# Hybrid Conformer and stick-breaking block: zero block kept in tiles, second convolution buffer, gate results on ScalarE's queue, last merged block by halves

## Chip, core and metric

The kernel runs on one core of a Trainium2 chip. The metric is the device time of one execution in microseconds (us), taken as the median of several runs. The kernel before takes 1413.03 us (three runs, 1412.89 to 1413.87).

Engines are named as in the profile: PE is TensorE (matmuls), PEld its weight loads, DVE is VectorE, ACT is ScalarE, POOL is GpSimd, SP is SyncE. Transfers are issued from the queues of SP and POOL in the kernel before, and all run on 16 DMA engines.

## What is computed

One layer of a decoder trunk on a sequence of 1024 tokens with 1024 channels, in float32. Each sub-layer is framed by RMSNorms and by a shift, scale and gate that come from a conditioning vector. The first sub-layer runs two mixers on the same input, merges them by gates, and projects:

```python
proj = h @ w_in
glu_in, qkv, gates = jnp.split(proj, [2 * CONV_WIDTH, 2 * CONV_WIDTH + 3 * ATT_WIDTH], axis=-1)
u_val, u_gate = jnp.split(glu_in, 2, axis=-1)
u = causal_depthwise_conv(u_val * jax.nn.sigmoid(u_gate), conv_w, conv_b)      # 31 taps
y_conv = jax.nn.silu(layernorm(u, conv_ln_g, conv_ln_b)) @ w_conv_out
o = stick_breaking_attention(q, k, v)                                          # 8 heads of 64
y_att = o @ w_att_out
g_conv, g_att = jnp.split(gates, 2, axis=-1)
merged = jax.nn.sigmoid(g_conv) * y_conv + jax.nn.sigmoid(g_att) * y_att
return merged @ w_o
```

Stick-breaking attention has a weight for each pair of a query t and an earlier key s (s < t, strictly): sigmoid of the score times the product of sigmoid(-score) over the keys between s and t. Weights of keys at or after the query are zero. The second sub-layer is a SwiGLU feed-forward block.

## The kernel before

All matmuls that need float32 accuracy are made of three: both operands are split into a high part in float32r and a low part (the rest), and high x high, high x low and low x high are summed in PSUM. A split is an ACT copy for the high part and a DVE subtraction for the low part. This pair of instructions stands behind nearly every operand.

The work runs in stages. The times are those of the profiled execution.

1. From 0 to about 75 us the input is normed and modulated, and the first projections are made as the operands arrive.
2. From about 75 to 430 us there is attention, with other projections as filler. Line 598 goes over four pairs of heads; each pair calls `glu` (line 417), `conv` for the group before (line 438) and `attend` (line 582), which runs `head` (line 514) twice and, between, `qk_pair` for the next pair. `head` has a higher priority, so the planner takes its instructions first and fills PE's time with the projections, the convolution and the plain gate (line 606).
3. Still inside the same scope come 14 early gate products. `early(i, q)` (line 615) computes for each of seven gate pairs two products that need only the modulated input, accumulated in one PSUM bank `k`; after the first (q = 0) and after the second (q = 1) an ACT instruction evicts the bank to a tile `ee` (tag `sg`, two buffers, line 623), and `store` (line 625) sends it to DRAM on POOL's queue. The second product of a pair adds to the bank, so it must follow the first eviction. The order is early(0, 0), early(1, 0), early(0, 1), early(2, 0) and so on.
4. From line 664 on, the rest of each gate pair is made in a form of Strassen's: sums of blocks of the modulated input, T1 to T4, are loaded again from DRAM (tiles `f`, `s`, `x`), combined on DVE (lines 674 to 677) and split (`make_t`, line 657). `other_five` (line 696) makes the five products of a pair from them. The convolution's LayerNorm (`ln_all`), its projection and the attention's projection follow.
5. At line 830 a loop over n = 0 to 7 merges the two mixers channel block by channel block. Each block has two halves of 512 tokens (c = 0, 1); for each half, DVE multiplies the projection by its gate and adds it to the convolution's part, tile `y`. After both halves the block of 1024 columns is split into `mhi` and `mlo` (line 842, `split_r`).
6. From line 954 the output projection `pwo` runs over these blocks for c = 0 first. From there on the FFN follows, up to the end at 1413 us; the change doesn't touch it.

**Order.** `TileContext(schedule_with_timeline_sim=True)` (line 1811) lets a planner set the order of the instructions on each engine: by priority, and by a modelled timeline of when operands and buffers are free. Two stretches of the code are pinned to the written order (`pin`, line 174: the start and the beginning of the FFN); the stages 2 to 5 are not. Each engine then runs its own list in order, so an instruction that waits holds all behind it on its engine. SP's and POOL's queues are such lists too.

**Diagonal blocks in `head`.** The 1024 x 1024 weights of a head are made by rows of queries: for each c (four per head) two query blocks of 128, ii = 0 and 1, over all keys up to them. For the product with the values the weights must be transposed, key by query, in steps of two key blocks (jp; jj = 0 and 1). Lines 559 to 576 do this for one step: four transposes of 128 x 128 on PE fill one PSUM bank `tr` of 512 columns, ACT evicts it to `ahi`, DVE writes the rest to `alo`, and four matmuls of 256 columns add to `av`. On the diagonal (jp = c), key block 1 lies after query block 0, so its weights are zero; the kernel transposes a tile of zeros there (line 564) to keep the layout:

```python
src = zeros if (jp == c and jj == 1 and ii == 0) else probs[ii][:, jo:jo + P]
```

There are 80 steps in all, 32 of them on the diagonal. `ahi` and `alo` have two buffers each.

**The convolution.** `glu(ct)` writes its product `u` to DRAM (`v_d`, line 436). `conv(ct)` (line 438) loads it back in another layout as `ph` (line 441), with four extra columns per group that POOL sets to zero (line 440), and runs 80 small matmuls `pcv` over it with five weight tiles `cvw` (tag `wraw`, three buffers). `ph` has one buffer, so the load for group ct waits until the products of group ct - 1 are through.

[...]

Of the kernel before, what the change touches and what calls it, by code (L numbers as in the profile page):

```python
# [69 lines left out]
def tile_block(ctx: ExitStack, tc: tile.TileContext, xT, vecs, ada1, ada2, win, wv, wcv, wat, wo, w1, w2, cvw, out):  # L70
# [29 lines left out]
    def store(dst, src):  # L100
        nc.gpsimd.dma_start(dst, src)
# [5 lines left out]
    make_identity(nc, ident)  # L107
    ones = small.tile([P, P], F32, name="ones")
    pool.memset(ones, 1.0)
    zeros = small.tile([P, P], F32, name="zeros")  # L110
    pool.memset(zeros, 0.0)
    eps = small.tile([P, 1], F32, name="eps")
    pool.memset(eps, EPS)

# [292 lines left out]
    with ExitStack() as sC:  # L407
        pc = mkpool(sC, "pc")
        with ExitStack() as sA:
# [4 lines left out]
            pool.memset(eye, 0.0)  # L414
            pool.tensor_copy(eye[:, CH - P:], ident)

            def glu(ct):
                u = pc.tile([P, T], F32, tag="u", name=f"u{ct}", bufs=1)
                u_mr = u.rearrange("p (r m) -> p m r", r=PH)
                sgs = list(sg0) if ct == 0 else []  # L420
                if ct:
                    w = load_w(win[4 + ct], f"wgg{ct}")
                    gb = banks2(f"pgg{ct}")
                    gemm(gb, w, h, range(KT))
                for c in range(NCH if ct else 0):
                    sg = sgp.tile([P, CH], F32, tag="sg", name=f"sg{ct}_{c}", bufs=2)
                    act.activation(sg, gb[c], AF.Sigmoid, bias=0.0, scale=1.0)
                    sgs.append(sg)
                w = load_w(win[ct], f"wgv{ct}")
                vb = banks2(f"pgv{ct}")  # L430
                gemm(vb, w, h, range(KT))
                for c in range(NCH):
                    ms = slice(c * (CH // PH), (c + 1) * (CH // PH))
                    vr, sr = (t.rearrange("p (m r) -> p m r", r=PH) for t in (vb[c], sgs[c]))
                    dve.tensor_tensor(u_mr[:, ms], vr, sr, op=ALU.mult)
                load(channels(v_d[ct]), u)

            def conv(ct):
                ph = pc.tile([P, NG, SH - 1 + TM], F32, tag="ph", name=f"ph{ct}", bufs=1)
                pool.memset(ph[:, :, 0:SH - 1], 0.0)  # L440
                load(ph[:, :, SH - 1:], v_d[ct].rearrange("g p m -> p g m"))
                wts = []
                for hf in range(2):
                    cv = bank(f"pcv{ct}_{hf}")
                    o = sgp.tile([P, NG // 2, TM], F32, tag="sg", name=f"co{ct}_{hf}", bufs=2)
                    for gi in range(NG // 2):
                        g = hf * (NG // 2) + gi
                        for d in range(SH):
                            n, at = divmod((g * SH + d) * P, T)
                            if n == len(wts):  # L450
                                wts.append(wp.tile([P, T], F32, tag="wraw", name=f"cvw{ct}_{n}"))
                                load(wts[n], cvw[ct, n])
                            pe.matmul(cv[:, gi * TM:(gi + 1) * TM], wts[n][:, at:at + P],  # L453
                                      ph[:, g, SH - 1 - d:SH - 1 - d + TM], start=(d == 0), stop=(d == SH - 1))
                    for gi in range(NG // 2):
                        b = C_CB + ct * NG + hf * (NG // 2) + gi
                        act.activation(o[:, gi], cv[:, gi * TM:(gi + 1) * TM], AF.Identity, bias=vec[:, b:b + 1],
                                       scale=1.0)
                    load(u_d[ct][hf * (NG // 2):(hf + 1) * (NG // 2)].rearrange("g p m -> p g m"), o)
# [54 lines left out]
            def head(p, hh, qst, kst, klo, vts, oT):  # L514
# [6 lines left out]
                for ci, c in enumerate(order):  # L521
# [5 lines left out]
                    for sc in range(nsc - 1, -1, -1):  # L527
                        probs = []
                        for i in (2 * c, 2 * c + 1):
                            W = P * (i + 1)  # L530
                            if i not in kaps:
                                kaps[i] = pa.tile([P, T], F32, tag="kap", name=f"ka{tag}_{i}", bufs=2)
                            kap = kaps[i]
                            s_lo, s_hi = sc * CH, min(W, (sc + 1) * CH)
                            w = s_hi - s_lo
                            beta = pa.tile([P, CH], F32, tag="beta", name=f"be{tag}_{i}_{sc}", bufs=4)
                            tcols = slice(i * P, (i + 1) * P)
                            z = psz.tile([P, CH], F32, tag="z", name=f"z{tag}_{i}_{sc}")
                            z_lo = s_lo if w >= 256 else max(0, s_hi - 256)
                            z_hi = max(s_hi, z_lo + 256)  # L540
                            zw, zo = z_hi - z_lo, s_lo - z_lo
                            diag = s_hi == W
                            pe.matmul(z[:, :zw], qst[:, tcols], kst[:, z_lo:z_hi], start=True, stop=False)
                            pe.matmul(z[:, :zw], qst[:, tcols], klo[:, z_lo:z_hi], start=False, stop=True)  # L544
                            act.activation(kap[:, s_lo:s_hi], z[:, zo:zo + w], AF.Sigmoid, bias=0.0, scale=-0.125)  # L545
                            m = w - 1 if diag else w
                            act.activation(beta[:, :m], z[:, zo:zo + m], AF.Sigmoid, bias=0.0, scale=0.125)  # L547
                            rev = kap[:, s_lo:s_hi][:, ::-1]
                            if diag:
                                pool.memset(beta[:, m:w], 0.0)  # L550
                                dve.tensor_tensor_scan(rev, rev, eye[:, CH - w:][:, ::-1], 0.0, op0=ALU.mult,  # L551
                                                       op1=ALU.add)
                            else:
                                dve.tensor_tensor_scan(rev, rev, rev, kap[:, s_hi:s_hi + 1], op0=ALU.mult,  # L554
                                                       op1=ALU.bypass)
                            dve.tensor_tensor(beta[:, :m], beta[:, :m], kap[:, s_lo + 1:s_lo + 1 + m], op=ALU.mult)  # L556
                            probs.append(beta)
                        for jp in range(min(c, 2 * sc + 1), 2 * sc - 1, -1):
                            tr = pst.tile([P, CH], F32, tag="tr", name=f"tr{tag}_{c}_{jp}")
                            for jj in range(2):  # L560
                                j = 2 * jp + jj
                                for ii in range(2):
                                    jo = (j - 4 * sc) * P
                                    src = zeros if (jp == c and jj == 1 and ii == 0) else probs[ii][:, jo:jo + P]
                                    o = jj * 256 + ii * P
                                    pe.transpose(tr[:, o:o + P], src, ident)  # L566
                            ahi = pa.tile([P, CH], F32R, tag="ahi", name=f"ahi{tag}_{c}_{jp}", bufs=2)
                            alo = pa.tile([P, CH], F32R, tag="alo", name=f"alo{tag}_{c}_{jp}", bufs=2)
                            act.activation(ahi, tr, AF.Copy)  # L569
                            dve.tensor_tensor(alo, tr, ahi, op=ALU.subtract)  # L570
                            for jj in range(2):
                                j = 2 * jp + jj
                                lhs = vts[j][:, hidx].rearrange("p a d -> p (a d)")
                                cols = slice(jj * 256, jj * 256 + 256)
                                pe.matmul(avc, lhs, ahi[:, cols], start=(jp == c and jj == 0), stop=False)  # L575
                                pe.matmul(avc, lhs, alo[:, cols], start=False, stop=(jp == 0 and jj == 1))  # L576
                    if ci % 2 == 1:
# [37 lines left out]
            def early(i, q):  # L615
# [6 lines left out]
                prod0(k, w, ("B11", "B21")[q], q == 0)  # L622
                e = sgp.tile([P, CH], F32, tag="sg", name=f"ee{q}_{i}", bufs=2)
                act.activation(e, k, (AF.Copy, AF.Sigmoid)[q])  # L624
                store(s_d[2 * i][:, :CH] if q else e_d0[i], e)

            for n, i in enumerate(GPAIRS):
                early(i, 0)
# [5 lines left out]
    with ExitStack() as sG:  # L634
# [90 lines left out]
        def split_r(src, names, hi_eng, lo_eng):  # L725
            hi, lo = (hp.tile([P, T], F32R, tag="act", name=nm) for nm in names)
            copy_to(hi_eng, hi, src)
            lo_eng.tensor_tensor(lo, src, hi, op=ALU.subtract)
            return hi, lo
# [100 lines left out]
        for n in range(KT):  # L830
# [6 lines left out]
            for c in range(NCH):  # L837
# [1 line left out]
                load(sg[c], s_d[8 + n][:, cs])  # L839
                last = dve.tensor_tensor(sg[c], yb[c], sg[c], op=ALU.mult)  # L840
                dve.tensor_tensor(y[:, cs], y[:, cs], sg[c], op=ALU.add)
            hi, lo = split_r(y, (f"mhi{n}", f"mlo{n}"), act, dve)
            mhi.append(hi)
            mlo.append(lo)
        assert not a2
        add_bias(16, 32)
        fold_gate(gpost1, 16, C_POST1)
# [968 lines left out]
```

## Time and profile before

| what | value |
|---|---|
| median of three runs | 1413.03 us (1412.89 to 1413.87) |
| profiled execution, its own time | 1414.92 us |
| its span | 1413.2 us, 18854 instructions |
| mean granted PE clock | 0.99 |
| DMA packets | 93789, 265.02 MB, mean 188 GB/s |
| SP's queue (hardware descriptors) | 201.68 MB, 42.0% of 16 engines |
| POOL's queue (software descriptors) | 62.14 MB, 12.4% of 16 engines |

The page has one line with the busy time of each engine, a row of forty slices of the span for each, and the groups of instructions that cost most. In a group's line stand the line of the code, the engine, the operation, output<-inputs by the program's names, shapes and count; then the busy time in us and the mean duration of one in ns; then the idle time of the engine in front of them and what ended it. In a timeline, the columns are start in us, duration in us, engine, line, operation and tiles; in square brackets stand the idle time in front of it and what ended that. The durations of matmuls are latencies: they overlap, and what one takes from PE is the step to the next start. The granted clock is the share of TensorE's full clock that was granted in a stretch.

### The profile page before, as it was taken

What the parts mean: (1) busy time and instruction counts of PE and PEld (TensorE: products, weight loads), DVE (VectorE), ACT (ScalarE), POOL (GpSimd) and SP (SyncE); (2) the same over time, 40 slices, a digit from 0 to 9 for tenths busy, and PEclk for the clock granted to TensorE, in tenths of its full rate; (3) what the DMA queues carried; (4) which work ended last, traced back from release to release, by engine and by line L of the source; (5) the groups of instructions that cost most, each with busy time, mean ns of one, the idle gap of its engine ahead of it and who ended that gap; (6) DMA issues with size and microseconds to landing.
All of it is one profiled execution on the core that took longest, in us unless ns stands there. A gap on an engine that the chain in (4) does not pass through costs nothing.

```text
span 1413.2 us, 18854 instructions
## 1 busy us (share of the span) xinstructions
PE 1378.3 (98%) x6810; PEld 1157.3 (82%) x6810; DVE 1048.3 (74%) x1591; ACT 655.3 (46%) x1146; POOL 117.4 (8%) x262
## 2 busy tenths in 40 slices
PE   7999999999998999999999999999999999999996
PEld 5898898998886788788877778888888887888886
DVE  7897687675865888878589878778877776785355
ACT  6375566364554455512356553334434443434441
POOL 0100001000001111000011110001111110000002
PEclk8999999999999999999999999999999999999998
DMA  9512051140348554973934545456777769586736
GB/s 382 200 39 82 16 164 30 46 150 30 120 150 298 208 170 148 349 226 124 360 120 163 182 148 177 165 171 212 260 250 246 264 240 387 177 337 221 254 116 120
DMA packets 93789, 265.02 MB, mean 188 GB/s; under 512 B 10048, under 2 KB 21440, under 8 KB 92672
## 3 DMA queue, kind: packets, MB, share of 16 engines
q1 hardware_dynamic: 74352, 201.68, 42.0%
q0 software_dynamic: 19344, 62.14, 12.4%
q8 instruction: 53, 0.87, 0.3%
q14 instruction: 40, 0.33, 0.1%
HBM read 192.74 MB, written 71.04 MB: 187 GB/s over the span
## 4 chain that ended last, share of the span: by engine, by line
PE 75%; issue 9%; DVE 8%; DMA 4%; ACT 2%; POOL 1%; SPq 0%; DVEq 0%; POOLq 0%; ACTq 0%
PE ka L982 14%; PE ka L1524 9%; PE kc L982 8%; PE pwo L900 6%; PE pb L1524 4%; PE pgv L168 3%; PE pv L473 3%; PE pgg L168 2%; PE pk L168 2%; PE pq L168 2%; PE ke L1090 2%; PE pcv L453 2%; PE tr L566 2%; PE pa L1524 2%; PE kb L982 2%
## 5 line engine op out<-in xcount | busy, mean ns | idle before, releaser
L545 ACT ACTIVATE ka<-z 128x128 f32<-128x128 f32 (+2 forms) x96 | 47.0, 496 | 55.8 <-PE z L544 51.9
L551 DVE TENSOR_TENSOR_SCAN ka<-ka,eye 128x128 f32<-128x128 f32 (+1 forms) x64 | 52.1, 831 | 23.2 <-ACT ka L545 23.0
L570 DVE TENSOR_TENSOR alo<-tr,ahi 128x512 fp32r<-128x512 f32 x80 | 53.4, 685 | 21.3 <-ACT ahi L569 20.7
L569 ACT ACTIVATE ahi<-tr 128x512 fp32r<-128x512 f32 x80 | 46.7, 603 | 39.1 <-PE av L575 22.9
L1524 PE MATMUL ka<-gt,w2f 128*128 128x512 f32 x264 | 63.4, 389 | 0.0
L556 DVE TENSOR_TENSOR be<-be,ka 128x127 f32<-128x127 f32 (+2 forms) x96 | 51.2, 550 | 12.1 <-ACT be L547 8.5
L1524 PEld LDWEIGHTS ka<-gt,w2f 128*128 128x128 f32 x264 | 49.5, 188 | 10.3
L123 DVE SCALAR_TENSOR_TENSOR ada<-ada,cb 128x1024 f32<-128x1024 f32 x32 | 38.9, 1223 | 23.6 <-DMA ada<-in_ada_dram 23.4
L1090 PE MATMUL ke<-b,w_hi 128*128 128x512 f32 x176 | 55.2, 395 | 0.0
L547 ACT ACTIVATE be<-z 128x127 f32<-128x127 f32 (+2 forms) x96 | 46.4, 496 | 17.8 <-PE tr L566 17.6
L566 PE MATMUL tr<-ident,be 128*128 128x128 f32 x288 | 46.6, 272 | 0.0
L453 PE MATMUL pcv<-ph,cvw 128*128 128x128 f32 x320 | 43.7, 282 | 2.5 <-DMA ph<-v_d 2.5
L554 DVE TENSOR_TENSOR_SCAN ka<-ka 128x512 f32<-128x512 f32 x32 | 40.4, 1274 | 6.3 <-ACT ka L545 6.3
L404 PE MATMUL k<-hhi,a 128*128 128x512 f32 x112 | 38.3, 413 | 6.6 <-ACT ee L624 6.6
L453 PEld LDWEIGHTS pcv<-ph,cvw 128*128 128x128 f32 x320 | 41.5, 198 | 3.5 <-issue 2.7
L575 PE MATMUL av<-ahi,vst 128*128 128x256 f32 x160 | 43.8, 291 | 0.0
L576 PE MATMUL av<-alo,vst 128*128 128x256 f32 x160 | 42.2, 290 | 0.0
L1090 PEld LDWEIGHTS ke<-b,w_hi 128*128 128x128 f32 x176 | 32.9, 188 | 7.9 <-issue 1.0
L147 ACT ACTIVATE gt<-X 128x512 fp32r<-128x512 f32 x33 | 20.3, 629 | 39.4 <-DVE X L1567 14.3
L473 PE MATMUL pv<-wv_hi,hhi 128*128 128x256 f32 x128 | 36.7, 287 | 1.6 <-DVE vst L478 0.9
L147 ACT ACTIVATE s1o<-s 128x512 fp32r<-128x512 f32 x22 | 13.8, 629 | 48.8 <-PE ka L982 41.0
L473 PE MATMUL pv<-wv_lo,hhi 128*128 128x256 f32 x128 | 36.3, 285 | 0.0
(545 smaller groups left out, 4145.8 us busy)
## 6 DMA issues: line engine op xcount, KB each, us to landing
w_d<-w2o POOLq DMA_DIRECT2D x44, 512.0 KB, 7.6
w2f<-w_d SPq DMA_DIRECT2D x44, 512.0 KB, 4.5
ada<-in_ada_dram SPq DMA_DIRECT2D x32, 512.0 KB, 5.7
w2r<-in_w_dram SPq DMA_DIRECT2D x44, 256.0 KB, 3.8
w1g<-in_w_dram SPq DMA_DIRECT2D x21, 512.0 KB, 3.7
w1u<-in_w_dram SPq DMA_DIRECT2D x21, 512.0 KB, 5.7
cvw<-in_cvw_dram SPq DMA_DIRECT2D x20, 512.0 KB, 3.8
ada_w<-in_ada_dram SPq DMA_DIRECT2D x8, 1024.0 KB, 13.9
```

Of the source, the lines that this page charges most:

```text
L168: pe.matmul(bank, st[:, cols], mv[k][:, c * CH:(c + 1) * CH], start=(i == 0 and s == 0), stop=(i == n - 1 and s == 2))
L453: pe.matmul(cv[:, gi * TM:(gi + 1) * TM], wts[n][:, at:at + P], ph[:, g, SH - 1 - d:SH - 1 - d + TM], start=(d == 0), stop=(d == SH - 1))
L473: pe.matmul(pv[:, :256], st[k][:, tcols], mv[:, wc], start=(k == 0 and i == 0), stop=(k == KT - 1 and i == 2))
L545: act.activation(kap[:, s_lo:s_hi], z[:, zo:zo + w], AF.Sigmoid, bias=0.0, scale=-0.125)
L551: dve.tensor_tensor_scan(rev, rev, eye[:, CH - w:][:, ::-1], 0.0, op0=ALU.mult, op1=ALU.add)
L556: dve.tensor_tensor(beta[:, :m], beta[:, :m], kap[:, s_lo + 1:s_lo + 1 + m], op=ALU.mult)
L566: pe.transpose(tr[:, o:o + P], src, ident)
L570: dve.tensor_tensor(alo, tr, ahi, op=ALU.subtract)
L900: pe.matmul(bank_, st[:, cols], mv[k][:, cs], start=(k == 0 and q == 0), stop=(k == KT - 1 and q == 2))
L982: pe.matmul(bank_, st[:, cols], t[:, mv], start=(first and j == 0 and s == 0), stop=(j == HK - 1 and s == 2), skip_group_check=not first)
L1090: pe.matmul(kbs[f], wes[f][st][:, cols], t[:, mv], start=(i == 0 and j == 0 and q == 0), stop=(j == HK - 1 and q == 2), skip_group_check=i ...
L1524: pe.matmul(dst, w[st][:, cols], g[mv], start=first and s == 0, stop=last and s == 2, skip_group_check=more)
```

## The change

Four things change in the kernel, and one setting of the program.

1. The tile of zeros goes. Two pairs of tiles (`dhi`, `dlo`) are kept for diagonal blocks alone, and POOL sets their first 128 columns to zero once. A diagonal step transposes three blocks instead of four, with the second key block in front (columns 0 to 255) and the first behind (256 to 511), so the zero block lies in columns 0 to 127; ACT and DVE write only columns 128 to 511. The four matmuls read all 512 columns as before. Diagonal steps take the two pairs in turn; the other steps have `ahi` and `alo` with two buffers each for themselves.
2. `ph` has two buffers.
3. The store of an early gate result is issued from ACT's queue instead of POOL's.
4. For the last merged block (n = 7), the split is made by halves: after each half's sum, ACT writes the high half and DVE the low half.
[...]

```diff
-    zeros = small.tile([P, P], F32, name="zeros")
-    pool.memset(zeros, 0.0)
...
+            kept = []
+            for i in range(2):
+                kept.append([pa.tile([P, CH], F32R, name=f"d{nm}{i}") for nm in ("hi", "lo")])
+                for t in kept[i]:
+                    pool.memset(t[:, :P].bitcast(F32), 0.0)
+            ndiag = count()
...
-                ph = pc.tile([P, NG, SH - 1 + TM], F32, tag="ph", name=f"ph{ct}", bufs=1)
+                ph = pc.tile([P, NG, SH - 1 + TM], F32, tag="ph", name=f"ph{ct}", bufs=2)
...
+                            new = slice(P if jp == c else 0, CH)
+                            at = (256, 0) if jp == c else (0, 256)
                             for jj in range(2):
                                 j = 2 * jp + jj
                                 for ii in range(2):
+                                    if jp == c and jj > ii:
+                                        continue
                                     jo = (j - 4 * sc) * P
-                                    src = zeros if (jp == c and jj == 1 and ii == 0) else probs[ii][:, jo:jo + P]
-                                    o = jj * 256 + ii * P
-                                    pe.transpose(tr[:, o:o + P], src, ident)
-                            ahi = pa.tile([P, CH], F32R, tag="ahi", name=f"ahi{tag}_{c}_{jp}", bufs=2)
-                            alo = pa.tile([P, CH], F32R, tag="alo", name=f"alo{tag}_{c}_{jp}", bufs=2)
-                            act.activation(ahi, tr, AF.Copy)
-                            dve.tensor_tensor(alo, tr, ahi, op=ALU.subtract)
+                                    o = at[jj] + ii * P
+                                    pe.transpose(tr[:, o:o + P], probs[ii][:, jo:jo + P], ident)
+                            if jp == c:
+                                ahi, alo = kept[next(ndiag) % 2]
+                            else:
+                                ahi = pa.tile([P, CH], F32R, tag="ahi", name=f"ahi{tag}_{c}_{jp}", bufs=2)
+                                alo = pa.tile([P, CH], F32R, tag="alo", name=f"alo{tag}_{c}_{jp}", bufs=2)
+                            act.activation(ahi[:, new], tr[:, new], AF.Copy)
+                            dve.tensor_tensor(alo[:, new], tr[:, new], ahi[:, new], op=ALU.subtract)
...
-                store(s_d[2 * i][:, :CH] if q else e_d0[i], e)
+                act.dma_start(s_d[2 * i][:, :CH] if q else e_d0[i], e)
...
+                if n < KT - 1:
+                    continue
+                if c == 0:
+                    mhi.append(hp.tile([P, T], F32R, tag="act", name=f"mhi{n}"))
+                    mlo.append(hp.tile([P, T], F32R, tag="act", name=f"mlo{n}"))
+                act.activation(mhi[n][:, cs], y[:, cs], AF.Copy)
+                dve.tensor_tensor(mlo[n][:, cs], y[:, cs], mhi[n][:, cs], op=ALU.subtract)
-            hi, lo = split_r(y, (f"mhi{n}", f"mlo{n}"), act, dve)
-            mhi.append(hi)
-            mlo.append(lo)
+            if n < KT - 1:
+                hi, lo = split_r(y, (f"mhi{n}", f"mlo{n}"), act, dve)
+                mhi.append(hi)
+                mlo.append(lo)
...
-    nc = bacc.Bacc("TRN2", target_bir_lowering=False, num_devices=1)
+    nc = bacc.Bacc("TRN2", target_bir_lowering=False, num_devices=1, dynamic_dma_scratch_size=8192)
```

More of the change, by code (lines that the diff above doesn't have):

```diff
@@ L573, in head @@
                                 lhs = vts[j][:, hidx].rearrange("p a d -> p (a d)")
-                                cols = slice(jj * 256, jj * 256 + 256)
+                                cols = slice(at[jj], at[jj] + 256)
                                 pe.matmul(avc, lhs, ahi[:, cols], start=(jp == c and jj == 0), stop=False)
```

## The prediction

> **What bounds the kernel now.** I read the page's shares first, then the stages, then what TensorE (PE) waits for, then the single places.
>
> ```profile
> PE 1378.3 (98%) x6810; PEld 1157.3 (82%) x6810; DVE 1048.3 (74%) x1591; ACT 655.3 (46%) x1146; POOL 117.4 (8%) x262
> ```
>
> PE is busy for 98% of the span. A time goes down here only if PE has less to do, or if one of its few gaps closes. The stages (columns: stretch, its length, then busy time of PE, PEld, DVE, ACT, POOL, then granted PE clock, DMA share, GB/s) show where the gaps are:
>
> ```profile
> 75.00:375.00 300.00, 299.13 (x1878) 269.04 (x1877) 224.83 (x323) 165.24 (x343) 10.07 (x56) 1.00 0.22 70
> 380.00:385.00 5.00, 2.46 (x20) 2.24 (x19) 4.53 (x6) 3.24 (x8) 0.00 (x0) 0.98 0.77 250
> 385.00:390.00 5.00, 5.00 (x32) 5.00 (x32) 1.53 (x4) 0.39 (x1) 0.00 (x0) 0.67 0.29 65
> 440.00:450.00 10.00, 8.25 (x36) 6.17 (x34) 7.17 (x12) 5.50 (x10) 1.08 (x2) 1.00 1.05 411
> 450.00:460.00 10.00, 6.04 (x24) 4.35 (x24) 10.00 (x17) 5.67 (x12) 1.08 (x2) 1.00 1.00 382
> 460.00:470.00 10.00, 9.07 (x28) 7.25 (x29) 10.00 (x17) 6.27 (x12) 2.15 (x4) 0.66 0.49 174
> ```
>
> The attention stage (75 to 375 us) is PE-bound without a hole: 299.13 of 300 us. After it come two holes, at 380 to 385 and at 440 to 461, and after each a stretch in which the granted clock is about two thirds. PE's own list of waits names them, and a third place:
>
> ```profile
> PE k L404 <- ACT ee L624: 6.6, 4, 4.0
> ...
> PE pcv L453 <- DMA ph<-v_d: 2.5, 1, 2.5
> ...
> PE pwo L900 <- ACT mhi L147: 1.3, 1, 1.3
> ```
>
> The change touches exactly these three waits, and a piece of PE's work in the attention stage.
>
> **The zero block.** Each of the 8 heads has 4 diagonal blocks, so 32 of the transposes in front of the value product only turn zeros around.
>
> ```profile
> L566 PE MATMUL tr<-ident,zeros x32: 270/272/273, 82.8 to 418.8; 128*128 128x128 f32 x32
> L111 POOL MEMSET zeros<- x1: 206/206/206, 1.0 to 1.0; 128x128 f32 x1
> ```
> ```profile
> 82.72 0.27 PE L566 MATMUL tr<-ident,be 128*128 128x128 f32 x1
> 82.83 0.27 PE L566 MATMUL tr<-ident,zeros 128*128 128x128 f32 x1
> 82.94 0.27 PE L566 MATMUL tr<-ident,be 128*128 128x128 f32 x1
> ```
>
> The duration of one (272 ns) is latency; what it takes from PE is the step between starts, 0.11 us. Removing 32 of them where PE has no gap is worth 32 x 0.11 = 3.5 us. The eviction to the high part (ACT) and the low part (DVE) shrinks from 512 to 384 columns for the diagonal blocks; both engines have slack there (DVE 224.83 and ACT 165.24 of 300 us), so I cost that at nothing, and it cannot be a loss. The kept tiles need four zero fills on GpSimd (POOL) at the start, about 4 x 206 ns by the row of the old fill; POOL is 8% busy and they come long before the first diagonal block. Without that cover they would cost 0.8 us. Diagonal and other blocks now rotate through two pairs of buffers each instead of sharing two: that takes waits from ACT, which PE doesn't wait for here, so nothing again.
>
> **The second convolution buffer.**
>
> ```profile
> 381.68 0.28 PE L544 MATMUL z<-klo,qst 128*128 128x256 f32 x1
> 384.49 2.38 PE L453 MATMUL pcv<-ph,cvw 128*128 128x128 f32 x11 [2.54 <-DMA ph<-v_d]
> ```
> ```profile
> 366.13 0.33 SPq L98 DMA_DIRECT2D v_d<-u  x1
> ...
> 379.03 0.38 SPq L98 DMA_DIRECT2D ph<-v_d  x1
> ```
> ```profile
> DMA to landing us min/median/max: 4.4/5.5/7.5
> ```
>
> The last group's values are stored at 366.13, but the load of its phases is issued only at 379.03, when the buffer is free, and needs some 5.5 us (the landing times of this tile). With a second buffer it can go out once the store has landed, about 369 to 370, and be there by 376. The gap of 2.54 us goes, and so does the slow clock behind it: 5.00 us at 0.67 are 5.00 x 0.33 = 1.7 us of work lost. Together 4.2 us. On SP's queue the load moves past the weight loads and the store that now stand between the two; they come later by its issue alone (0.38 us), and the products of the group before, which use them, have none of PE's waits. What is late next is the weights of the third convolution chunk, which wait for a buffer that the same products free; those move up with them. Bounds: 2.5 us if the clock dips anyway, 4.2 if all goes. I take 4.2, because the dip follows the gap directly.
>
> [...]
>
> **The early gate results on ACT's queue.** Fourteen results (tile ee, two buffers) are evicted by ACT and stored through POOL's queue; a buffer is free when its store has landed.
>
> ```profile
> L624 ACT ACTIVATE ee<-k 128x512 f32<-128x512 f32 x14 | 8.0, 589 | 9.7 <-DMA e_d<-ee 3.3 <-DMA s_d<-sg 2.5 <-DMA s_d<-ee 2.3
> ```
> ```profile
> 458.99 0.74 DVE L677 SCALAR_TENSOR_TENSOR f<-f,mod,f 128x512 f32<-128x512 f32 x1
> ...
> 459.77 0.63 ACT L147 ACTIVATE T4o<-f 128x512 fp32r<-128x512 f32 x1 [0.80 <-DVE f L677]
> ...
> 460.30 1.07 ACT L624 ACTIVATE ee<-k 128x512 f32<-128x512 f32 x2
> ...
> 460.93 0.80 PE L404 MATMUL k<-hhi,a 128*128 128x512 f32 x1 [4.01 <-ACT ee L624]
> ```
> ```profile
> e_d<-ee POOLq DMA_DIRECT2D x7, 256.0 KB, 5.7
> s_d<-ee POOLq DMA_DIRECT2D x7, 256.0 KB, 4.1
> ...
> u_d<-co SPq DMA_DIRECT2D x8, 256.0 KB, 4.9
> ...
> out_dram<-yc SPq DMA_DIRECT2D x4, 256.0 KB, 2.4
> ```
> ```profile
> L101 POOL DMA_DIRECT2D e_d<-ee x7: 542/542/543, 435.2 to 475.8; - x7
> ```
> ```profile
> L98 SPq DMA_DIRECT2D v_d<-u x4: 326/328/331, 120.7 to 366.1; - x4
> ```
>
> Of PE's 6.6 us, 4.01 are one gap: the eviction stands on ACT behind four splits (T2, T1, T3, T4) that wait for a DVE with no slack (10.00 of 10 us). It stands there because the order is planned from a modelled timeline, in which its buffer wasn't free earlier. The other 2.6 us follow a landing directly. The slow clock behind the long gap costs 9.07 x 0.34 = 3.1 us, so the place holds 6.6 + 3.1 = 9.7 us.
>
> ACT's queue isn't used in the trace. Nearest is SP's: 256 KB land in 2.4 to 4.9 us, against 4.1 to 5.7 on POOL. One result is due each 2.72 us (12 products in 2.72 us, below), so with two buffers a buffer may be held for 5.4 us. On POOL it was held 0.59 + 0.54 + 5.7 = 6.8 us; on a queue like SP's 0.59 + 0.33 + 2.4 to 4.9 = 3.3 to 5.8 us, mostly inside. I take it that the landing stalls go and that the planner sets the evictions ahead of the splits.
>
> But not all 9.7 us arrive. The next stage needs the last T2 split, at the end of the chain on the full DVE, and PE is covered by what is left of the k products:
>
> ```profile
> L660 DVE TENSOR_TENSOR T2o<-f,T2o x4: 685/687/689, 448.5 to 467.1; 128x512 fp32r<-128x512 f32 x4
> ```
> ```profile
> 472.10 5.44 PE k L404 x24
> 479.81 2.72 PE k L404 x12
> ```
>
> After the first T2 product 5.44 + 2.72 = 8.2 us of k work are left. If PE gains more than that it has nothing to do until T2 is split, so the wait moves there. The term is 8.2 us; bounds 0 (below) and 9.7.
>
> On ACT, 14 stores at 0.33 us (SP's issue) are 4.6 us; ACT has 5.50 + 5.67 + 6.27 = 17.4 of 30 us busy from 440 to 470. Behind each store on ACT wait the splits for DVE and PE. With the slack as cover, nothing; without it, the second rival.
>
> **The last merged block by halves.**
>
> ```profile
> 669.54 1.29 DVE L841 TENSOR_TENSOR yc<-yc,sga 128x512 f32<-128x512 f32 x2
> ...
> 671.95 1.23 DVE L728 TENSOR_TENSOR mlo<-yc,mhi 128x1024 fp32r<-128x1024 f32 x1 [1.12 <-ACT mhi L147]
> ```
> ```profile
> 670.87 1.06 ACT L147 ACTIVATE mhi<-yc 128x1024 fp32r<-128x1024 f32 x1 [3.88 <-DVE yc L841]
> ```
> ```profile
> 671.97 0.73 PE L900 MATMUL pwo<-mhi,wo_hi 128*128 128x512 f32 x2 [1.27 <-ACT mhi L147]
> ```
>
> ACT can begin after the first of the two adds, 0.6 us sooner, and half a block takes about 0.6 instead of 1.06 us: 1.1 of the 1.27 us. The low half then needs one DVE step of about 0.7 us in place of 1.23. One more instruction on each engine adds a few tenths; I take 1.0 us (bounds 0 and 1.27).
>
> [...]
>
> **Sum.** 3.5 + 4.2 + 8.2 + 1.0 = 16.9 us off the span of 1413.2 us. The profiled execution took 1414.92 us in all, 1.7 more than its span; the median of the runs is 1413.03, all but equal to the span, so I take the sum from the median: 1396.1 us. Since all the work up to about 480 us is ordered anew from the modelled timeline, I allow 3 us either way; own range 1392 to 1400.
>
> **Rivals.**
> *The early stalls stay.* The stage from 440 to 460 moves 411 and 382 GB/s with the DMA engines at 1.00 and over, so a store may land no sooner from another queue; SP's 4.9 us speaks for it, 2.4 us against. Then only 3.5 + 4.2 + 1.0 = 8.7 us, 1404.3 us; with the issue saved (0.21 us on 7 stores per buffer, 1.5 us) 1402.8.
> [...]
>
> *Slower: ACT becomes the path.* A store on ACT waits for the end of the eviction in front of it (at most its 0.59 us) and then issues (0.33 us as on SP, 0.54 as on POOL): 14 of them hold ACT for 4.6 to 15.8 us, in front of the splits that feed the full DVE. If 13 us of that land on the T chain and the 9.7 us stay too, the other terms (8.7 us) are overdrawn by 4: 1417 us. It decides once more than 8.7 us of hold stand in that chain. Against it: even 15.8 us over the 50 us of the stage, 9.5 per 30, bring ACT only from 17.4 to 27 of 30.
>
> *Nothing gained.* The new order opens a gap elsewhere of the size of the one at 456.5 to 460.9 (4.0 + 3.1 = 7.1 us); two of these eat the gain: 1410 to 1414 us. For it: the order isn't pinned there. Against: from 75 to 375 us there is always other work ready.
>
> **How the numbers follow.** Forecast 0.52; early stalls stay 0.32 (1400 to 1407); nothing gained 0.08; ACT the path 0.05; more than the sum 0.03 (below 1391). The range 1391 to 1407 leaves out the last three. A measurement of this kernel tells about 0.2%, 2.8 us, from no change. Faster 0.87, same 0.08, slower 0.05.
>
> **What would show it.** Right: no transposes of zeros; no wait of pcv for ph, its load issued near 370 us; clock near 1.0 all through 375 to 480; ee stores on ACT's queue with landings under 4.9 us and no wait of k for ee; a short wait of PE for T2 instead; pwo's gap under 0.3 us. Wrong: PE gaps of some microseconds between 400 and 480 with ACT as releaser, a DMA issue in front of them on ACT, or PE below 299 of 300 us in the attention stage.

## The result and the profile after

The changed kernel takes 1400.8 us (median of five runs, 1399.13 to 1401.73). Beside it the kernel before took 1413.87 us (five runs, 1412.89 to 1416.73). The ratio is 0.9908, 95% interval 0.9892 to 0.9924: 13.1 us faster, where the forecast had 16.9. It misses the forecast of 1396.1 us by 4.7. It lies just outside the forecast's own range of 1392 to 1400 us and inside the wider one of 1391 to 1407 us, which takes in the rival "the early stalls stay" (1404.3, or 1402.8 with the issue saved). So the total alone can't choose between the two; the runs of the single parts do. The profiled execution took 1400.80 us with a span of 1399.0 us. Of the experiments, one execution each of `u_zero`, `u_queue` and `e_buffers` took 1723, 7283 and 2727 us, far above the others, and is left out of the times and ratios below.

The page's line of shares, of the kernel after:

```profile
PE 1370.6 (98%) x6778; PEld 1150.3 (82%) x6778; DVE 1043.6 (75%) x1592; ACT 651.5 (47%) x1147; POOL 109.4 (8%) x251
```

PE has 32 matmul records fewer (6810 before), as the 32 transposes of zeros are gone. PE's waits in the stretches of the change, from the list of waits of the kernel after (total, number, longest):

```profile
PE pyc L747 <- ACT wc_hi L145: 2.1, 1, 2.1
PE k L402 <- ACT ee L635: 1.6, 1, 1.6
...
PE ka L402 <- DVE s2o L389: 0.8, 1, 0.8
```

Gone are the wait of `pcv` for `ph` and that of `pwo` for `mhi`. The wait of `k` for `ee` shrank from 6.6 us in four to 1.6 in one. A wait of 2.1 us of the convolution's projection (`pyc`) for its weights' high part (`wc_hi`) is new. The stretches of the kernel after, in the columns used for those of before:

```profile
75.00:375.00 300.00, 298.53 (x1865) 267.06 (x1864) 223.85 (x327) 164.29 (x349) 10.25 (x58) 1.00 0.23 72
375.00:430.00 55.00, 54.93 (x343) 48.87 (x342) 39.92 (x61) 31.19 (x68) 2.78 (x10) 1.00 0.70 224
380.00:385.00 5.00, 5.00 (x44) 4.86 (x44) 4.79 (x10) 3.63 (x11) 0.18 (x2) 1.00 0.69 189
385.00:390.00 5.00, 5.00 (x44) 4.92 (x43) 4.79 (x7) 3.47 (x8) 0.20 (x2) 1.00 0.43 138
430.00:440.00 10.00, 8.39 (x38) 6.62 (x37) 9.96 (x17) 6.48 (x13) 0.00 (x0) 1.00 0.98 356
440.00:450.00 10.00, 10.00 (x46) 8.29 (x45) 6.42 (x10) 6.63 (x12) 0.00 (x0) 1.00 0.79 266
450.00:460.00 10.00, 10.00 (x46) 8.29 (x45) 6.21 (x10) 3.98 (x7) 0.00 (x0) 1.00 0.81 269
460.00:470.00 10.00, 10.00 (x44) 7.93 (x43) 7.12 (x12) 3.99 (x7) 0.00 (x0) 1.00 0.84 289
```

The clock is 1.00 in every one of them; the stretches 385 to 390 and 460 to 470 had 0.67 and 0.66 before. PE's 298.53 us in the first row (299.13 before) are below the 299 that the prediction named as a sign of being wrong, though by 0.5 us only. There is more in the second row than the closed hole at 381 us. Here is the same stretch of the kernel before:

```profile
375.00:430.00 55.00, 52.46 (x331) 47.55 (x330) 32.81 (x47) 29.12 (x64) 2.65 (x13) 0.97 0.44 140
```

DVE does 39.92 us of work there after, 32.81 before. The work is not more; it comes sooner. The attention's last transposes and the first instructions of the T chain show it. The answers by tile, of the kernel after, give first and last start (tile `tr`, then `T2o`):

```profile
L574 PE MATMUL tr<-ident,be x288: 270/272/276, 82.6 to 403.0; 128*128 128x128 f32 x144
...
  PE av L586: 10.6, 6
```
```profile
L671 DVE TENSOR_TENSOR T2o<-f,T2o x4: 678/685/691, 423.0 to 443.0; 128x512 fp32r<-128x512 f32 x4
```

and the kernel before has, for tile `tr`:

```profile
L566 PE MATMUL tr<-ident,be x288: 270/272/277, 82.4 to 418.9; 128*128 128x128 f32 x144
...
  PE av L575: 22.9, 10
```

The attention starts at the same time and issues its last transposes 15.9 us sooner; `T2o` begins at 423.0 in place of 448.5 us. The row "PE av" is the idle time that the evicting engine spent until the value product had read a buffer: 22.9 us in 10 waits before, 10.6 in 6 after.

What ties the T chain to the attention's end is SP's queue. The chain's first operands, the loads of `f`, come right behind the store of the attention's last output, `o_d<-oT`. Before, and then after:

```profile
432.07 0.33 SPq L98 DMA_DIRECT2D o_d<-oT  x1
...
433.41 11.90 SPq L98 DMA_DIRECT2D f<-xm_d  x14
```
```profile
410.20 0.33 SPq L98 DMA_DIRECT2D o_d<-oT  x1
...
412.70 9.49 SPq L98 DMA_DIRECT2D f<-xm_d  x14
```

In all 14 traces of this study the first load of `f` is issued 0.4 to 2.5 us after that store. So the two new pairs of buffers let the attention run ahead of the filler work, its last output is stored 21.9 us sooner, and DVE begins the T chain while PE still has other products. The prediction gave these buffers nothing.

The load of `ph` is issued at 367.03 us, behind its store at 364.41, and the loads of `ph` land in 4.0 to 4.8 us; the prediction had an issue at 369 to 370 us and a landing of 5.5. SP's queue in the kernel after:

```profile
364.41 0.33 SPq L98 DMA_DIRECT2D v_d<-u  x1
367.03 0.37 SPq L98 DMA_DIRECT2D ph<-v_d  x1
```

The early gate stores, tile `ee` of the kernel after:

```profile
L636 ACTq DMA_DIRECT2D e_d<-ee x7: 326/327/361, 430.0 to 457.8; - x7
L636 ACTq DMA_DIRECT2D s_d<-ee x7: 326/326/330, 437.8 to 465.5; - x7
...
DMA to landing us min/median/max: 2.0/4.3/6.9
```

They are on ACT's queue at 0.33 us each, but land in 4.3 us (median) and up to 6.9, little sooner than before (5.3 and 7.2).

### The profile page after: what moved, and what is told of

It reads as the page before. It is cut to its first block, busy times and chain, and to the rows that moved or that the text cites. A ratio compares the mean times of both kernels' runs of the same rounds, so it can differ in the third digit from the quotient of the medians.

```text
span 1399.0 us, 18714 instructions
## 1 busy us (share of the span) xinstructions
PE 1370.6 (98%) x6778; PEld 1150.3 (82%) x6778; DVE 1043.6 (75%) x1592; ACT 651.5 (47%) x1147; POOL 109.4 (8%) x251
## 4 chain that ended last, share of the span: by engine, by line
PE 76%; issue 14%; DVE 3%; DMA 3%; ACT 2%; POOL 1%; POOLq 0%; DVEq 0%; SPq 0%; ACTq 0%
PE ka L1001 14%; PE ka L1543 9%; PE kc L1001 8%; PE pwo L919 5%; PE pb L1543 4%; PE pgv L166 3%; PE pyc L747 3%; PE pya L166 3%; PE pv L478 3%; PE pq L166 2%; PE pk L166 2%; PE pgg L166 2%; PE pa L1543 2%; PE kb L1001 2%; PE tr L574 2%
## 5 line engine op out<-in xcount | busy, mean ns | idle before, releaser
L580 ACT ACTIVATE ahi<-tr 128x512 fp32r<-128x512 f32 x48 | 28.3, 600 | 23.1 <-PE tr L574 17.4
L581 DVE TENSOR_TENSOR alo<-tr,ahi 128x512 fp32r<-128x512 f32 x48 | 32.3, 684 | 8.5 <-ACT ahi L580 8.3
L574 PEld LDWEIGHTS tr<-ident,be 128*128 128x128 f32 x288 | 34.8, 140 | 2.8
L402 PE MATMUL k<-hhi,a 128*128 128x512 f32 x112 | 35.4, 391 | 1.7 <-ACT ee L635 1.6
L478 PE MATMUL pv<-wv_hi,hlo 128*128 128x256 f32 x128 | 36.7, 287 | 0.0
```

Source lines behind the costliest of these rows:

```text
L478: pe.matmul(pv[:, :256], st[k][:, tcols], mv[:, wc], start=(k == 0 and i == 0), stop=(k == KT - 1 and i == 2))
L574: pe.transpose(tr[:, o:o + P], probs[ii][:, jo:jo + P], ident)
```

## The experiments

Two theories were set against each other. Theory S is the prediction's sum: each part is worth its own term (3.5, 4.2, 8.2, 1.0). Theory O says that the queue gives 0 to 2 us, as in the rival where the early stalls stay, and that the early end of the attention, brought about by the zero block's edit, makes up for it. A ratio compares a kernel with executions of the kernel before beside it (their medians were 1413.10, 1413.31 and 1414.05 us in the three sets), and can differ a little from the quotient of the two medians. Where a ratio is turned into us below, it is the distance from 1 times 1413. All kernels of the experiments are built with `dynamic_dma_scratch_size=8192`, the one setting of the program in the diff (the expectations call it the descriptor memory), so that it was measured alone as well.

**Each part alone.** `e_zero` takes only the zero block of the diff (kept tiles, three transposes, 384 columns):

```diff
+if jp == c and jj > ii:
+    continue
...
+ahi, alo = kept[next(ndiag) % 2]
...
+act.activation(ahi[:, new], tr[:, new], AF.Copy)
+dve.tensor_tensor(alo[:, new], tr[:, new], ahi[:, new], op=ALU.subtract)
```

> [...] Theory S (each part is worth its own term): 32 x 0.11 = 3.5 us less, ratio 0.9975. Theory O (the new order matters more than the terms): the profile after had moved ahead by only 1.2 us at 347 us, where some 26 zero transposes were gone (2.9 us), so small gaps open in the attention stage and this part alone brings 1 to 2 us by then; and if the early end of the attention stage (tr ends 16 us sooner after the change) comes from this part, the gaps at 381 and 456 us change too, and the kernel gains 6 us or more.

Measured: 1407.3 us, ratio 0.9955 (0.9939 to 0.9971), 6.4 us faster, as theory O had it (6 or more) and not S (3.5). `e_phase`:

```diff
-name=f"ph{ct}", bufs=1)
+name=f"ph{ct}", bufs=2)
```

> The second convolution buffer alone (descriptor memory 8 KB). Theory S: 4.2 us less (gap of 2.5 us and the slow clock behind it), ratio 0.997; the early gaps at 443 to 461 us stay (6.6 us). Theory O: the gap at 381 us goes, but the time is given back or more is won in the early gates, since the attention stage ends at another time: anything but 4 us, with a changed wait of k for ee.

Measured: 1408.42 us, 0.9967 (0.9955 to 0.9979), 4.7 us faster. The wait of `pcv` is gone and the clock dip with it (1.00 from 380 to 390 us); the 6.6 us of `k` for `ee` stay. The term of 4.2 stands. `e_queue`:

```diff
-store(s_d[2 * i][:, :CH] if q else e_d0[i], e)
+act.dma_start(s_d[2 * i][:, :CH] if q else e_d0[i], e)
```

> The early gate stores on ACT's queue alone (descriptor memory 8 KB). Theory S: the wait of k for ee (6.6 us) and the slow clock behind it go, 8.2 us less, ratio 0.994. Theory O (the stores land hardly sooner, median 4.3 us after the change against 5.3; the early gaps went because the DVE chain of T splits started earlier): 0 to 2 us less, and a wait of k for ee of 4 us or more stays.

Measured: 1411.03 us, 0.9995 (0.9982 to 1.0009): no difference that can be told from zero, where S had 8.2 us (the quotient of the medians, 0.9985, would be 2.1 us). Its list of waits, and its tile `ee`, say why:

```profile
PE k L404 <- ACT ee L624: 3.8, 4, 2.3
PE ka L404 <- ACT s2o L147: 2.5, 2, 1.7
PE pcv L453 <- DMA ph<-v_d: 2.5, 1, 2.5
```
```profile
L625 ACTq DMA_DIRECT2D e_d<-ee x7: 326/327/345, 434.5 to 477.7; - x7
L625 ACTq DMA_DIRECT2D s_d<-ee x7: 326/326/328, 442.7 to 484.6; - x7
...
  DMA e_d<-ee: 4.4, 3
...
DMA to landing us min/median/max: 2.0/5.7/7.9
```

The stores land in 5.7 us, no sooner than from POOL's queue (5.3): the evictions still wait 4.4 + 2.5 + 0.3 = 7.2 us for landings, against 3.3 + 2.5 + 2.3 = 8.1 before. PE keeps 3.8 of its 6.6 us, just under the 4 that theory O named, and nearly all it gains (2.5 of 2.8 us) it waits for `s2o`, the split weights of later products. That is what the prediction's rival had expected: in this trace the other queue saves the issue alone, with 0.33 beside 0.54 us of issue and 5.7 beside 5.3 us of landing. `e_half` takes only the halves of the last block:

```diff
+act.activation(mhi[n][:, cs], y[:, cs], AF.Copy)
+dve.tensor_tensor(mlo[n][:, cs], y[:, cs], mhi[n][:, cs], op=ALU.subtract)
...
-hi, lo = split_r(y, (f"mhi{n}", f"mlo{n}"), act, dve)
+if n < KT - 1:
+    hi, lo = split_r(y, (f"mhi{n}", f"mlo{n}"), act, dve)
...
```

> The last merged block by halves alone (descriptor memory 8 KB). Theory S: 1.0 to 1.5 us less, ratio 0.999; pwo's gap of 1.27 us gone. Theory O: the same, since the order ahead of it doesn't change; only what stands behind it can.

Measured: 1413.13 us, 1.0002 (0.999 to 1.0015): nothing that shows, though 1.0 us would lie within its error of 1.8. `e_memory`:

```diff
-nc = bacc.Bacc("TRN2", target_bir_lowering=False, num_devices=1)
+nc = bacc.Bacc("TRN2", target_bir_lowering=False, num_devices=1, dynamic_dma_scratch_size=8192)
```

> The descriptor memory of 8 KB alone. The order of all five engines is that of before, instruction by instruction. Both theories: no difference (within 1.5 us, the spread of the runs), POOL's issues stay at 542 ns. A rival in which POOL waits for room: issues above 542 ns and a wait on POOL that wasn't there.

Measured: 1414.15 us, 1.0005 (0.999 to 1.0019): nothing. In the kernels that have this setting and the `ee` stores on POOL's queue, an issue takes 540 to 543 ns (`e_zero`, `e_buffers`, `e_four`, `u_queue`), beside 542 to 543 before. The engines of `e_memory` run the same instructions in the same order as those of the kernel before, so it is a second look at that kernel, and it shows where the halves' gain may have gone. In its timeline ACT splits the last block whole, and PE takes it up:

```profile
666.40 1.06 ACT L147 ACTIVATE mhi<-yc 128x1024 fp32r<-128x1024 f32 x1 [3.70 <-DVE yc L841]
```
```profile
667.73 0.39 PE L900 MATMUL pwo<-mhi,wo_lo 128*128 128x512 f32 x1
667.96 0.62 PE L900 MATMUL pwo<-mhi,wo_hi 128*128 128x512 f32 x2
```

The split ends at 666.40 + 1.06 = 667.46 us, PE's next product starts 0.23 us after the one before it, without a gap. The gap of 1.27 us on which the prediction's term rested is in the trace of before and in none of the other kernels that split the last block whole (`e_memory`, `e_phase`, `e_queue`, `e_zero`, and later `e_buffers` and `e_four`): of the two executions of this very order, one has it. So it comes and goes with the execution and is no fixed part of the kernel's time.

**The change without one part.** `u_zero` is the change with the old four transposes and shared buffers:

```diff
-if jp == c and jj > ii:
-    continue
...
-ahi, alo = kept[next(ndiag) % 2]
...
+src = zeros if (jp == c and jj == 1 and ii == 0) else probs[ii][:, jo:jo + P]
+pe.transpose(tr[:, o:o + P], src, ident)
```

> The change without the zero block (tile of zeros back, four transposes). Theory S: 3.5 us over the changed kernel, about 1404 us, ratio to before 0.993. Theory O: if the early end of the attention stage comes from the zero block, the early gaps come back in part and it stands at 1406 us or above.

Measured: 1409.49 us, 0.9965 (0.995 to 0.998). Beside 0.9908 for the whole, the zero block is worth 0.0057, or 8 us, in the change. Its trace has the stores on ACT's queue and still a wait of 4.7 us of `k` for `ee`, and `T2o` begins at 445.2 us. `u_phase` puts back the one buffer for `ph`:

```diff
-name=f"ph{ct}", bufs=2)
+name=f"ph{ct}", bufs=1)
```

> The change with one convolution buffer. Theory S: 4.2 us over the changed kernel, about 1405 us, ratio 0.994, with a wait of pcv for ph of about 2.5 us. Theory O: the attention stage ends late again, the T chain starts late, and more than 4.2 us are lost, 1406 us or above.

Measured: 1406.17 us, 0.9944 (0.9923 to 0.9964): the second buffer is worth 0.0036, or 5 us. But there is no wait of `pcv` for `ph` in its trace, which neither theory expected. The longest gap is another:

```profile
434.12 0.50 PE L402 MATMUL k<-hhi,a 128*128 128x512 f32 x1 [3.58 <-ACT ee L635]
```

With the zero block the order changes so that the old gap is covered. In this one trace the price seems to be paid at an early gate product instead (3.58 us, where the changed kernel has 1.6 to 1.7); how a late `ph` leads to it was not followed. `u_queue` puts the stores back on POOL's queue:

```diff
-act.dma_start(s_d[2 * i][:, :CH] if q else e_d0[i], e)
+store(s_d[2 * i][:, :CH] if q else e_d0[i], e)
```

> The change with the early stores on POOL's queue as before. Theory S: 8.2 us over the changed kernel, about 1409 us, ratio 0.997, with a wait of k for ee of some 6 us. Theory O: most of the gain stays without ACT's queue, 1401 to 1404 us, with a wait of k for ee under 3 us.

Measured: 1402.67 us, 0.9913 (0.9891 to 0.9935), beside 0.9908 for the whole: the queue gives 0.7 us, within the error of 3.8. From its waits and its tile `ee`:

```profile
PE k L402 <- ACT ee L635: 2.1, 1, 2.1
PE pyc L747 <- ACT wc_hi L145: 2.1, 1, 2.1
```
```profile
L101 POOL DMA_DIRECT2D e_d<-ee x7: 540/540/543, 428.5 to 457.7; - x7
...
DMA to landing us min/median/max: 2.3/3.6/6.8
```

Without the new queue, too, PE waits only 2.1 us for `ee`, and the landings are 3.6 us. The loads of `f` are out of the way by then: the DMA share from 440 to 460 us is 0.68 here, 0.80 in the changed kernel and 1.02 before. So the wait of 6.6 us shrank because the attention ends sooner, not because the stores go out elsewhere. The zero block alone leaves 4.2 us of it (below), so the second `ph` buffer seems to help as well; one trace of each can't settle the shares. Theory O stands for the queue in both directions.

**What in the zero block's edit does it.** It has two sides: 32 transposes less, and four more buffers with smaller evictions. `e_buffers` adds buffers to the kernel before and changes nothing else:

```diff
-ahi = pa.tile([P, CH], F32R, tag="ahi", name=f"ahi{tag}_{c}_{jp}", bufs=2)
-alo = pa.tile([P, CH], F32R, tag="alo", name=f"alo{tag}_{c}_{jp}", bufs=2)
+ahi = pa.tile([P, CH], F32R, tag="ahi", name=f"ahi{tag}_{c}_{jp}", bufs=4)
+alo = pa.tile([P, CH], F32R, tag="alo", name=f"alo{tag}_{c}_{jp}", bufs=4)
```

> The kernel before with four buffers for the high and the low transposed weights in place of two, with the smaller descriptor memory, and with all four transposes of a diagonal step. The zero block alone measured 0.9955 of before (-6.4 us), 3.5 us of which 32 steps of 0.11 us explain. Theory B (the rest comes from the added buffers): about -2.9 us, ratio 0.998, and z ends more than 10 us sooner than before. Theory C (the rest comes from the new order or from the smaller evictions of the diagonal steps): within 1 us of before, ratio 0.9995 to 1.0005, with z ending about where it did.

`e_four` is `e_zero` with the transposes of zeros put back, into columns that nobody reads:

```diff
...
-if jp == c and jj > ii:
-    continue
 jo = (j - 4 * sc) * P
 o = at[jj] + ii * P
-pe.transpose(tr[:, o:o + P], probs[ii][:, jo:jo + P], ident)
+src = zeros if (jp == c and jj > ii) else probs[ii][:, jo:jo + P]
+pe.transpose(tr[:, o:o + P], src, ident)
```

> The zero block alone, but PE still turns the block of zeros around, into columns of the bank that nobody reads: 32 transposes more than with the zero block alone, the kept tiles and the smaller evictions as there. If the 32 steps cost what the prediction says (0.11 us each), it is 3.5 us above the zero block alone: -2.9 us from before, ratio 0.998. If the whole gain is the transposes: 1.000. If the kept tiles and smaller evictions make all of it, as the early end of attention suggests: 0.9955, with z ending 15 us or more sooner than before as there.

Measured: `e_buffers` 1409.98 us, 0.997 (0.9956 to 0.9985), 4.2 us faster; `e_four` 1406.51 us, 0.9951 (0.9934 to 0.9969), 6.9 us faster and no slower than `e_zero` without the 32 transposes (difference -0.0004 with a half-width of 0.0024 from the two intervals: -0.6 us, 3.3 either way). Both traces end the attention early. Tile `tr` of `e_buffers`:

```profile
L566 PE MATMUL tr<-ident,be x288: 270/272/329, 85.9 to 412.5; 128*128 128x128 f32 x144
...
  PE av L575: 6.6, 3
```

It starts 3.5 us later than in the kernel before (85.9 against 82.4; the reason is at the end) and still issues its last 6.4 us sooner, and the wait for the value product falls from 22.9 to 6.6 us, with nothing but buffers. The score products `z`, which the expectations name, end at 400.4 us here and at 397.0 in `e_four`, against 412.2 before, and `T2o` begins at 434.6 and 429.4 us. So theory B stands: the added buffers are worth 4 us by themselves (2 to 6 by the interval), in a stage in which PE has no hole. Theory C, that buffers alone do nothing, is out.

The second kernel shows that the 32 steps are not worth their 3.5 us in the time, though only just: the error reaches to 2.7 us. Where they may have gone can be read from the waits of `e_four` and of `e_zero`, in this order, in one execution of each:

```profile
PE k L404 <- ACT ee L636: 2.6, 3, 1.2
```
```profile
PE k L402 <- ACT ee L635: 4.2, 2, 2.6
...
PE pyc L747 <- ACT wc_hi L145: 2.1, 1, 2.1
```

and from the 4 us behind the longest gap of `e_zero`:

```profile
434.12:438.12 4.00, 4.00 (x11) 3.23 (x12) 3.02 (x5) 0.44 (x1) 1.07 (x2) 0.62 0.91 349
```

The plan of `e_zero` has 4.2 - 2.6 = 1.6 us more of waits for `ee`, a clock of 0.62 behind one of them (4.00 x 0.38 = 1.5 us) and the 2.1 us of `pyc`: 5.2 us against the 3.5 saved. On this reading the transposes do come off PE, and the order that the planner makes of the shorter work gives the time back in stages that PE then waits in. That these gaps recur in other executions is not shown, and how much another order would keep was not tried.

**A third buffer, and the whole change again.** `x_three` is the change with three buffers for the tiles of tag `sg`, of which `ee` is one; it makes the same edit at the other tiles of the tag:

```diff
...
-e = sgp.tile([P, CH], F32, tag="sg", name=f"ee{q}_{i}", bufs=2)
+e = sgp.tile([P, CH], F32, tag="sg", name=f"ee{q}_{i}", bufs=3)
...
```

> The whole change with three buffers for the gate tiles (sg, ee, co, cb) in place of two. Theory O (what is left of k's wait for ee is one eviction held behind a wait on ACT or a landing): the wait of 1.6 us goes and with it at most 2 us, ratio 0.990 down to 0.9895. If the order is planned anew to its disadvantage: 0.991 or more. The prediction's queue term (8.2 us for the queue alone) says nothing is left here: 0.991.

`whole` is the changed kernel without any edit, on the same chip.

> The whole change once more, on the same chip as the three beside it: 0.9908 of before as at first; the profiled span may lie several us from the first one's 1399.0 us, as it did in the parts, without its median moving. The places of PE's waits should be the same: 1.6 us of k for ee, 2.1 us of pyc for wc_hi, none of pcv for ph and of pwo for mhi.

Measured: `whole` 1401.76 us, 0.9914 (0.9897 to 0.993), with `k` waiting 1.9 us in two and `pyc` 2.1 us; `x_three` 1397.72 us, 0.989 (0.9873 to 0.9906). Of PE's waits in these stretches `x_three` keeps one of note, and `k` waits for no `ee` any more:

```profile
PE pyc L747 <- ACT wc_hi L145: 2.1, 1, 2.1
```

The difference of the two is 0.0024 with a half-width of 0.0023 from their intervals, 3.4 us, more than the 2 expected and just clear of its error. `x_three` is the fastest kernel of this study. A third buffer does what the other queue was meant to do: it lets the bank be evicted while two stores are still under way. The evictions of `ee` wait 0.7 us for landings in its trace, against 3.8 + 1.0 + 0.3 = 5.1 in the changed kernel, though the landings take no less (4.8 us, against 4.3). A third buffer with the stores on POOL's queue was not tried.

## Why the prediction was right, and where it wasn't

The total came out nearer than its terms, by luck: two errors lay on opposite sides. Term by term (us; the half-widths are those of the ratios):

| part | predicted | alone | taken out of the change |
|---|---|---|---|
| zero block | 3.5 | 6.4 ± 2.3 | 8 |
| second `ph` buffer | 4.2 | 4.7 ± 1.7 | 5 |
| stores on ACT's queue | 8.2 | 0.7 ± 1.9 | 0.7 |
| last block by halves | 1.0 | -0.3 ± 1.8 | not tried |
| `dynamic_dma_scratch_size=8192` | no term | -0.7 ± 2.0 | not tried |
| sum | 16.9 | 10.8 | measured for the whole: 13.1 |

- **The failed step: "I take it that the landing stalls go and that the planner sets the evictions ahead of the splits", 8.2 us.** The term is mis-sized by some 7.5 us. The stores on ACT's queue landed in 5.7 us alone and 4.3 in the change, against 5.3 on POOL's and 3.6 with the change's other parts. SP's rows of 4.9 and 2.4 us were of other stages, with less traffic (a DMA share of 0.31 from 190 to 402 us and of 0.62 from 1407 to 1412); the stretch's own share of 1.05 and 1.00, which the prediction gave for the rival, was the better guide. The rival's account of the queue (0 to 1.5 us) was right about the queue and wrong about the place: the wait of 6.6 us went down to 1.6 for another reason.
- **The zero block, "so nothing again" for the buffers.** The argument was that ACT's waits for a buffer cost nothing where PE doesn't wait. PE's busy share of the stage was indeed no issue (299.13 of 300 before), but the buffers let the attention end 15.9 us sooner, so that DVE's chain for the next stage starts 25.5 us sooner (448.5 to 423.0) and the holes behind it shrink. The term of 3.5 us measured 6.4 alone, and its source is another: the 3.5 us of transposes don't show in the time, and what the prediction put at nothing brings all of it, 4.2 us with buffers alone and 6.9 with kept tiles and smaller evictions (`e_four`). The two are 2.7 us apart with a half-width of 3.2, so what the smaller evictions add stays open.
- **The second `ph` buffer.** Right in mechanism and size: no wait for `ph`, load at 367 us, clock 1.00 from 380 to 390. In the change the old gap would have been covered without it, and its 5 us seem to come from a gap of 3.58 us further on; if so, the term was right there by luck.
- **The halves.** Whether the mechanism works is not shown. The gap is not in the trace of after, but it is in no other trace with a whole split either: it is in the one of `before` and not in that of `e_memory`, which has the same order. One profile shows which gaps can occur, not which do as a rule.
- **The T2 chain as the next wait.** The prediction put it at a short wait for T2. There is none: what came are waits for split weights, `s2o` (0.84 us at 527.8, and 1.73 us at 551.8 in `e_queue`) and `wc_hi` (2.1 us at 556.5). All lie 80 us or more behind the last T2 (443.0, and 467.4 in `e_queue`). The split to `wc_hi` stands on ACT behind the convolution's LayerNorm, which waits for DVE; in the kernel after:

```profile
554.31 0.63 ACT L795 ACTIVATE hhi<-lm 128x512 fp32r<-128x512 f32 x1 [1.69 <-DVE lm L793]
...
555.36 1.04 ACT L145 ACTIVATE wc_hi<-wc_raw 128x1024 fp32r<-128x1024 f32 x1
```

- **ACT as the path, and nothing gained.** ACT is busy for 6.63, 3.98 and 3.99 of 10 us in the stretches from 440 to 470, and the 14 stores add 14 x 0.33 = 4.6 us from 430 to 466; neither rival came.

## What to carry to other kernels

A stage in which one engine is full can still be improved by buffers on the engines beside it, if it has priority work and filler: here, with PE busy for 299.13 of 300 us, buffers alone gave 4.2 us (`e_buffers`), the priority work ended sooner and the next stage's slow chain got its start earlier. Before a wait for a store is cured by another queue, look at what the DMA engines do in that stretch: here, with a share of 1.05 and 1.00, another queue alone gave 0.7 ± 1.9 us, and on top of the change another buffer gave 3.4. And a gap of a microsecond from a single profiled execution is worth a second look at the unchanged kernel before it goes into a sum.

## What the runs showed of the hardware

**Behind a gap of 1.8 to 2.6 us the clock fell in some executions and not in others.** In the 14 profiled executions (those of before and after, and of the experiments), PE had 17 gaps of 1.0 to 1.8 us between 75 and 600 us, and none was followed by a lower clock in the next 4 us; 8 of 2.6 to 4.0 us, and all were (0.50 to 0.65); and 13 between 1.8 and 2.6 us, of which four were (0.57 behind 2.54, 2.47 and 1.84 us, 0.69 behind 2.08). Three of these four are among the four gaps in front of `pcv`, and one among the nine elsewhere, so the place may count as well as the length. At the same place in the same code it went both ways. First the stretch behind a gap of 2.41 us in `e_memory`, then behind 1.84 us in `e_half`:

```profile
385.00:390.00 5.00, 4.71 (x42) 4.74 (x43) 2.70 (x5) 0.51 (x2) 0.10 (x1) 1.00 0.52 171
```
```profile
385.00:390.00 5.00, 5.00 (x33) 5.00 (x32) 2.23 (x5) 0.38 (x1) 0.00 (x0) 0.66 0.34 97
```

What decides between the two outcomes in the middle group, no run here shows. The prediction's row, 0.67 from 385 to 390 us behind 2.54 us, is one of the four that fell.

**The same kernel varies by several us, in the two traces of it through the clock of its first 50 us.** `after` and `whole` are one kernel, with spans of 1399.0 and 1402.6 us. The stretch from 30 to 40 us, in `after` and then in `whole`, has most of the difference:

```profile
30.00:40.00 10.00, 10.00 (x46) 8.39 (x45) 9.89 (x15) 3.97 (x6) 1.07 (x2) 0.80 1.03 425
```
```profile
30.00:40.00 10.00, 10.00 (x33) 8.45 (x33) 9.89 (x15) 3.85 (x6) 1.07 (x2) 0.50 1.02 422
```

At 0.50 in place of 0.80, PE does 10.00 x 0.30 = 3.0 us less in it, and the attention's first transposes start at 85.9 in place of 82.6 us. `e_buffers` had the same late start. The six executions of `whole` fall in line with their mean granted clock: 1398.3 to 1401.0 us of span at 0.992, 1402.6 and 1404.0 at 0.989 and 0.988. Only these two executions of the kernel have a trace, so that the others differ for the same reason is likely and not shown. A part's worth is therefore taken here from medians of several executions, and a profile says only where the gaps lie.
